# A hybrid decoder step on one core: each delta head as three streams, with a fifth raw projection in the prologue

## The chip, the cores and the metric

The kernel runs on 1 core of a Trainium2 chip. The metric is the device time of one execution in microseconds (us). Five engines work side by side, each with its own in-order queue of instructions: PE (TensorE, matmuls), DVE (VectorE), ACT (ScalarE), POOL (GpSimd) and SP (SyncE, which here only issues DMAs).

## What is computed

One decoder layer on a prompt of 1024 tokens and 8 single-token samples, which the kernel treats as 1032 columns side by side. All is float32. The part that the change touches is branch A, a gated delta rule in 4 heads of 128 by 128, in chunks:

```python
h = rmsnorm(x, norm_g)
aq, ak, av, abeta, aalpha, agate, bu, bv, bgate, cq, cgate, mg = split(h @ w_in)
q, k, v = silu(causal_conv(aq, ak, av))          # 4 taps; q and k are then L2-normed per head
# per head, per chunk (gc = cumulative log decay):
L    = strictly_lower((k * beta) @ k.T * decay)
Tinv = inverse(I + L)                            # unit lower triangular
u, w = Tinv @ (v * beta), Tinv @ (k * beta * exp(gc))
attn = lower(q @ k.T * decay)
def step(S, c):                                  # over the chunks, one after another
    v_new = u[c] - w[c] @ S
    o     = q_dec[c] @ S + attn[c] @ v_new
    return S * g_last[c] + k_dec[c].T @ v_new, o
ya = rmsnorm(o) * silu(agate)
# branches B (spatial MLP on bu, bv, bgate) and C (attention into a memory), then
y = x + (g0 * (ya @ w_a) + g1 * (yb @ w_b) + g2 * (yc @ w_c)) @ w_out   # g = sigmoid(mg + b)
```

Here the chunks have 128 tokens, 8 to a head. The samples' tokens update eight separate states per head (`state_delta`).

## The kernel before

**Projections.** Each column tile of `w_in` (1024 x 128) is a job of PE: `project` runs three float32r products (`whi` x `hTh`, `whi` x `hTl`, `wlo` x `hTh`, which together replace one float32 product) over 8 blocks of depth and 3 column groups of 344, 72 matmuls in all (line L302). ACT and DVE split each weight tile into hi and lo (L277, L280) one job ahead. `plan_a` lists the jobs by name: k, v, q and ag (gate) of the four delta heads, bu, bv, bg of branch B, and gate tiles of the final merge. `plan_c` and `plan_m` follow in later stages.

**What sets the order.** The program is written out by one thread of Python. After every 6 matmuls of a projection `tick()` lets each running generator (`run.add`) go one step, up to its next `yield`; `yield n` skips n ticks. So the instructions of a generator stand in the queues between those of the projections that run at that point, and each engine executes its queue in that order. `run.until` runs generators on until a condition holds.

**Prologue.** Tiles k0, v0, bv0 and q0 are projected from x times g that isn't yet scaled by the root mean square (`raw_group`, four column groups of 256 or 264); DVE multiplies each result by `rbc`, the reciprocal root, on the way out. Then `n_again` splits the scaled h into hi and lo, and the small product for beta and alpha (L652, L653) is the first to use it.

**Delta heads.** `delta_all` runs `gates_gen`, then `delta_gen(h)` for the heads one after another. A head waits for its k, v and q (projection and convolution; the convolution of q runs on POOL, L485 and L487). Then, in this order: transposes of k (L225), E (decay), `LA` (L872: K·K and K·Q of a chunk in one matmul of 256 columns; L873 scales); the four diagonal 32x32 blocks of L go through DRAM (`ld` L883, `Lt` L887) into a layout in which POOL inverts them all at once, in 31 steps of two operations each (L926, L932); `sample_gen(h)` starts before that loop, so its load of `st` (L733) does as well; r (scaled v), the transposes of q and their squares follow. The inverse goes back through DRAM (`ud` L938, `U` L940); after `yield 14`, DVE transposes its blocks (`TA` L943) and small matmuls (from L951) build the full inverse U. Then come the recurrence over 8 chunks (L990 to L1006), the norm, and the turning back (transposes of `r`, DVE L1019 ahead of them). The kernel goes on to branches B and C when head 3 is done.

**Samples.** `sample_gen(h)` norms the samples' q and k, loads `st` (the eight states), multiplies them by q and k on PE, and sends d through DRAM (`ddr` L794, `dbc` L796) to update the states.

Of the kernel before, what the change touches and what calls it, by code (L numbers as in the profile page):

```python
# [151 lines left out]
def tile_mixer_step(ctx: ExitStack, tc: tile.TileContext, a):  # L152
# [576 lines left out]
    def sample_gen(h):  # L729
        kq, vs = kq_s[h]  # L730
# [90 lines left out]
    def delta_gen(h):  # L821
        while not {("k", h), ("v", h), ("q", h), "gates"} <= done:
            yield
        yield 1
        kq, vt = kq_t[h], v_t[h]
        kqs = sm.tile([P, 2, NB], F32, tag="kqs", name="kqs")
        G.tensor_copy(out=kqs, in_=kq[:, :, T:NT])
        vss = sm.tile([P, NB], F32, tag="vss", name="vss")
        G.tensor_copy(out=vss, in_=vt[:, T:NT])
        kq_s[h] = (kqs, vss)  # L830
        gcb = dp.tile([P, CC, P], F32, tag="gcb", name="gcb")
        SP.dma_start(out=gcb, in_=gcd[h * CC:(h + 1) * CC].rearrange("c i -> (c i)").partition_broadcast(P))
        E = dp.tile([P, CC, P], F32, tag="E", name="E")
        ss = sm.tile([P, 2, CC], F32, tag="ss", name="ss")
        Kg = dp.tile([P, CC, P], F32, tag="Kg", name="Kg")
        kd = dp.tile([P, CC, P], F32, tag="kd", name="kd")
        r = dp.tile([P, CC, P], F32, tag="r", name="r")
# [3 lines left out]
        nk = sm.tile([P, CC], F32, tag="nk", name="nk")  # L841
        halves = [slice(0, 4), slice(4, 8)]
        kt = []
        for cs in halves:
            t = dl().rearrange("p (c n) -> p c n", c=4)
            kt.append(t)
            for c in range(4):
                cc = cs.start + c
# [4 lines left out]
            V.tensor_tensor(out=Kg[:, cs], in0=t, in1=bc4(eg[:, h, cs]), op=ALU.mult)
            yield 1
        for c in range(CC):
            V.scalar_tensor_tensor(
                out=E[:, c], in0=gcb[:, c], scalar=gc[:, h, c:c + 1], in1=mask, op0=ALU.subtract, op1=ALU.add
            )
# [8 lines left out]
        yield
        LA = dp.tile([P, 2, CC, P], F32, tag="LA", name="LA")
        for c in range(CC):
            t = dl()[:, :256].rearrange("p (t i) -> p t i", t=2)  # L870
# [1 line left out]
            PE.matmul(t, lhsT=kq[:, 0, sl], rhs=kq[:, :, sl], start=True, stop=True)  # L872
            V.scalar_tensor_tensor(  # L873
                out=LA[:, :, c], in0=t, scalar=cj[:, c:c + 1],
                in1=E[:, c].unsqueeze(1).to_broadcast([P, 2, P]), op0=ALU.mult, op1=ALU.mult,
            )
# [4 lines left out]
        ld = dr.tile([CC, 4, 32, 32], F32, tag="ld", name="ld", bufs=2)
        for b in range(4):
            SP.dma_start(out=ld[:, b].rearrange("c j i -> j c i"), in_=LA[bsl[b], 0, :, bsl[b]])  # L883
# [8 lines left out]
        for cs, t in zip(halves, kt):  # L892
            V.tensor_tensor(out=kd[:, cs], in0=t, in1=bc4(ck[:, cs]), op=ALU.mult)
            yield
        yield from rsqrt_slow(nk, ssk, "nk")
        V.tensor_tensor(out=nk, in0=nk, in1=ssk, op=ALU.mult)
        run.add(sample_gen(h))
        for cs in halves:
            t = dl().rearrange("p (c n) -> p c n", c=4)
            for c in range(4):  # L900
                cc = cs.start + c
                transpose(t[:, c], vt[:, cc * P:(cc + 1) * P])
            V.tensor_tensor(out=r[:, cs], in0=t, in1=bc4(nk[:, cs]), op=ALU.mult)
            yield
        qg = kq[:, 1, :T].rearrange("p (c i) -> p c i", c=CC)
        for cs in halves:
            t = dl().rearrange("p (c n) -> p c n", c=4)
            for c in range(4):
                cc = cs.start + c
                transpose(t[:, c], qg[:, cc])  # L910
            for c in range(4):
                cc = cs.start + c
                S.activation(out=junk(), in_=t[:, c], func=AF.Square, accum_out=ss[:, 1, cc:cc + 1])
            yield 1
        V.tensor_tensor(out=gcb, in0=qg, in1=gcb, op=ALU.mult)
        yield
        ssq = sm.tile([P, CC], F32, tag="ssq", name="ssq")
        V.tensor_scalar(out=ssq, in0=ss[:, 1], scalar1=EPS, scalar2=None, op0=ALU.add)
        rq = sm.tile([P, CC], F32, tag="rq", name="rq")
        yield from rsqrt_slow(rq, ssq, "rq")  # L920
        V.tensor_scalar(out=rq, in0=rq, scalar1=DKS, scalar2=None, op0=ALU.mult)
        yield 2
# [14 lines left out]
        for q in range(4):
            SP.dma_start(out=udv[:, q], in_=X[bsl[q]])  # L938
        for b in range(4):
            SP.dma_start(out=U[bsl[b], :, bsl[b]], in_=ud[:, b].rearrange("c m q i -> (m q) c i"))  # L940
# [9 lines left out]
        for c in range(CC):  # L950
            PE.matmul(t1[b1, c], lhsT=LA[b0, 0, c, b1], rhs=TA[b0, c, b0], start=True, stop=True)  # L951
# [36 lines left out]
        for c in range(CC):  # L988
# [613 lines left out]
```

## Time and profile before

| | us |
|---|---|
| median of 3 runs (lowest to highest) | 1160.41 (1159.37 to 1164.16) |
| profiled execution, its own time | 1163.22 |
| its span | 1161.5 |
| PE busy in the span | 1119.0 (96%) |
| DVE busy | 637.7 (55%) |
| ACT busy | 412.2 (35%) |
| POOL busy | 230.8 (20%) |

The span runs from the first instruction to the last; the execution's own time is 1.7 us longer. PE's busy share says how much of the span no change of the other engines can take away. A row of the timeline gives the start, the duration, the engine (SPq is SP's queue of DMA issues), the line, the operation with output and input, and, in brackets, the idle time before it and what ended it. A row with xN stands for N instructions in succession; since matmuls are pipelined, the price of one is the distance from the start of its row to the start of the next, divided by N.

### The profile page before, as it was taken

The page shows a single profiled execution, that of the slowest core. Times are in us where ns is not written, and L with a number is a line of the kernel's source. Part 1 is how long each engine was busy: PE and PEld are TensorE (multiplying, and loading weights), DVE is VectorE, ACT ScalarE, POOL GpSimd, SP SyncE. Part 2 cuts the span into 40 slices and gives each one's busy share as a digit, 9 for nine tenths or more (in the row PEclk, how much of TensorE's full clock was granted, in tenths as well). Part 3 has the DMA queues.
Part 4 walks back from the last instruction along what each step waited for, and adds up shares of the span by engine and source line. Part 5 has one row for each costly group of instructions (what it writes and reads, how often), then busy time and mean ns, then how long its engine had stood idle before and what let it go on. Part 6 is the DMA issues. An engine that isn't in the chain of part 4 may idle for free.

```text
span 1161.5 us, 19130 instructions
## 1 busy us (share of the span) xinstructions
PE 1119.0 (96%) x7530; PEld 1070.1 (92%) x7530; DVE 637.7 (55%) x1585; ACT 412.2 (35%) x879; POOL 230.8 (20%) x392
## 2 busy tenths in 40 slices
PE   8959999999999999999899999999999999999997
PEld 8948999999999999999799999989999999998884
DVE  5993763477357635722386522645645256786554
ACT  6334332333332233333344323545445321232232
POOL 0043285036504540420034100101101000000000
PEclk8979999999999999999999999899999999999999
DMA  9103321233023302431644455344343365662221
GB/s 366 48 19 75 114 82 39 93 115 93 28 94 114 83 20 93 133 119 55 216 135 140 151 164 193 112 132 127 110 128 92 123 195 178 218 216 92 90 92 56
DMA packets 83033, 137.75 MB, mean 119 GB/s; under 512 B 21744, under 2 KB 51664, under 8 KB 82296
## 3 DMA queue, kind: packets, MB, share of 16 engines
q1 hardware_dynamic: 69392, 95.62, 25.3%
q10 hardware_dynamic: 13552, 40.92, 11.8%
q8 instruction: 59, 0.97, 0.4%
q14 instruction: 30, 0.25, 0.1%
HBM read 104.97 MB, written 31.64 MB: 118 GB/s over the span
## 4 chain that ended last, share of the span: by engine, by line
PE 84%; DVE 8%; DMA 4%; ACT 2%; issue 1%; SPq 0%; ACTq 0%; POOL 0%; DVEq 0%
PE pj L302 49%; PE dl L302 21%; PE tp L225 1%; PE dl L225 1%; PE dl L872 1%; DVE xT L330 1%; PE dl L1220 1%; DMA x<-mem_prompt 1%; PE dl L1006 1%; PE tp L1172 1%; PE dl L982 1%; PE dl L990 1%; PE dl L997 1%; DMA sbg<-g 1%; PE dl L1005 1%
## 5 line engine op out<-in xcount | busy, mean ns | idle before, releaser
L302 PE MATMUL pj<-hTh,whi 128*128 128x344 f32 (+1 forms) x1392 | 273.8, 331 | 9.6 <-DVE ql L188 3.4
L302 PE MATMUL pj<-hTh,wlo 128*128 128x344 f32 (+1 forms) x1392 | 267.1, 326 | 0.0
L302 PE MATMUL pj<-hTl,whi 128*128 128x344 f32 (+1 forms) x1392 | 260.1, 325 | 0.0
L302 PEld LDWEIGHTS pj<-hTh,whi 128*128 128x128 f32 x1392 | 225.3, 191 | 13.9 <-DVE ql L188 3.6
L302 PEld LDWEIGHTS pj<-hTh,wlo 128*128 128x128 f32 x1392 | 225.7, 190 | 1.9 <-issue 1.2
L302 PEld LDWEIGHTS pj<-hTl,whi 128*128 128x128 f32 x1392 | 226.7, 191 | 0.8 <-issue 0.2
L280 DVE TENSOR_TENSOR wlo<-raw,whi 128x1024 fp32r<-128x1024 f32 (+1 forms) x92 | 100.5, 1094 | 44.4 <-ACT whi L277 44.2
L277 ACT CAST whi<-raw 128x1024 fp32r<-128x1024 f32 (+1 forms) x92 | 86.1, 936 | 75.4 <-PE dl L302 64.9
L926 POOL TENSOR_TENSOR itmp<-X,Lt 128x60 f32<-128x60 f32 (+24 forms) x124 | 48.7, 393 | 174.0 <-DMA Lt<-ld 164.7
L1045 ACT COPY stg<-pj 128x344 f32<-128x344 f32 x72 | 32.1, 446 | 121.4 <-PE pj L302 121.3
L1277 POOL TENSOR_TENSOR kvt<-kvt,qb 128x1024 f32<-128x1024 f32 x8 | 19.2, 2418 | 214.6 <-DMA kvt<-cache_mem_v 214.6
L302 PE MATMUL dl<-yl,whi 128*128 128x344 f32 x288 | 57.2, 320 | 0.0
L302 PE MATMUL dl<-yh,wlo 128*128 128x344 f32 x288 | 57.1, 320 | 0.0
L302 PE MATMUL dl<-yh,whi 128*128 128x344 f32 x288 | 56.9, 319 | 0.0
L932 POOL TENSOR_TENSOR X<-X,itmp 128x60 f32<-128x60 f32 (+24 forms) x124 | 54.3, 438 | 9.7
L302 PEld LDWEIGHTS dl<-yl,whi 128*128 128x128 f32 x288 | 47.6, 188 | 0.0
L302 PEld LDWEIGHTS dl<-yh,whi 128*128 128x128 f32 x288 | 47.5, 188 | 0.0
L302 PEld LDWEIGHTS dl<-yh,wlo 128*128 128x128 f32 x288 | 47.4, 188 | 0.0
L994 DVE COPY y<-dl 128x128 f32<-128x128 f32 x32 | 9.3, 291 | 61.3 <-PE dl L992 40.1
L1460 DVE TENSOR_TENSOR stg<-dl,stg 128x344 f32<-128x344 f32 x48 | 24.7, 514 | 17.7 <-PE dl L302 17.7
L487 POOL TENSOR_TENSOR kq<-kq,cvt 128x512 f32<-128x512 f32 x24 | 33.4, 1392 | 1.9
L516 ACT COPY xraw<-pj 128x344 f32<-128x344 f32 x27 | 12.0, 444 | 59.9 <-PE pj L302 59.9
(389 smaller groups left out, 1669.6 us busy)
## 6 DMA issues: line engine op xcount, KB each, us to landing
raw<-w_tiles ACTq DMA_DIRECT2D x62, 512.0 KB
gate<-stg SPq DMA_DIRECT2D x23, 516.0 KB
stg<-gate SPq DMA_DIRECT2D x23, 516.0 KB
raw<-w_br ACTq DMA_DIRECT2D x24, 256.0 KB
x<-x_prompt SPq DMA_DIRECT2D x8, 512.0 KB
kvt<-cache_mem_k SPq DMA_DIRECT2D x16, 256.0 KB
kvt<-cache_mem_v SPq DMA_DIRECT2D x16, 256.0 KB
wor<-w_out SPq DMA_DIRECT2D x8, 512.0 KB
```

The lines of the kernel that those rows point to most:

```text
L225: PE.transpose(out, in_, ident[:p, :p])
L277: S.copy(out=hi, in_=raws[i])
L280: eng.tensor_tensor(out=lo, in0=raws[i], in1=f32(hi), op=ALU.subtract)
L302: PE.matmul(out, lhsT=w, rhs=r, start=(i == 0), stop=(i == len(ops) - 1))
L330: V.scalar_tensor_tensor(out=x[:, k], in0=x[:, k], scalar=colv[:, col + k:col + k + 1], in1=r, op0=ALU.mult, op1=ALU.mult)
L487: G.tensor_tensor(out=d[:, cs], in0=d[:, cs], in1=o, op=ALU.add)
L516: S.copy(out=raw[:, 3 + sl.start:3 + sl.stop], in_=o)
L926: G.tensor_tensor(out=tm, in0=X[:, 0:m, j:j + 1].to_broadcast([P, m, n]), in1=Lt[:, j:j + 1, j + 1:32].to_broadcast([P, m, n]), op=ALU.mult,)
L932: G.tensor_tensor(out=X[:, 0:m, j + 1:32], in0=X[:, 0:m, j + 1:32], in1=tm, op=ALU.subtract)
L1045: project("gate", i, lambda n, sl, o: S.copy(out=t[:, sl], in_=o))
L1277: G.tensor_tensor(out=kts[hb], in0=kts[hb], in1=qb[:, hb * 4:hb * 4 + 4].unsqueeze(2).to_broadcast([P, 4, 2, P]), op=ALU.mult,)
L1460: V.tensor_tensor(out=sg[:, sl], in0=o, in1=sg[:, sl], op=ALU.mult)
```

## The change

`delta_gen` is cut in three generators. `inverse_gen(h)` waits for k alone. It computes K·K (L860, two-pass float32 of 128 columns) into `L`; the squares of k, which ACT summed from the transposed k, are now the diagonal of K·K (DVE multiplies by the identity and reduces). Then come E, L, `ld`, `Lt`, POOL's loop (L901, L907), `ud`, `U` and the small matmuls (from L929). `chunks_gen(h)`, started ahead of the loop, does the transposes of k, K·Q (L998) into `A`, the transposes of q and v. `chain_gen(h)` does the recurrence and the turning; when it starts, `inverse_gen(h + 1)` starts as well. Flags ("dbc", "rec", "turned", "chunks") keep the buffers of two heads apart: `Lt` takes the buffer of the samples' `dbc`, the diagonals that of `p2`. `sample_gen(h)` is added after POOL's loop instead of before it. k, v and q of a head are projected only when the chunks of the head before are done.

`plan_a` is put in another order, with 8 gates at the end instead of 1 + 7. In the prologue a fifth tile, bv1, is projected from x g in the four column groups of the others, and `n_again` moves behind q0 into bv1's loop.

```diff
@@ plan_a
-        [("k", 0), ("v", 0), ("bv", 0), ("q", 0), ("ag", 0), ("bv", 1), ("bv", 2)],
-        [("k", 1), ("v", 1), ("q", 1), ("ag", 1), ("bv", 3), ("bg", 0), ("bu", 0)] + gates(1),
-        [("k", 2), ("v", 2), ("q", 2), ("ag", 2), ("bg", 1), ("bu", 1), ("bg", 2), ("bu", 2)],
-        [("k", 3), ("v", 3), ("q", 3), ("ag", 3), ("bg", 3), ("bu", 3)] + gates(7),
+        [("k", 0), ("v", 0), ("bv", 0), ("q", 0), ("bv", 1), ("ag", 0), ("bv", 2), ("bv", 3), ("bg", 0)],
+        [("k", 1), ("v", 1), ("q", 1), ("bu", 0), ("ag", 1), ("bg", 1), ("bu", 1)],
+        [("k", 2), ("v", 2), ("q", 2), ("bg", 2), ("ag", 2), ("bu", 2), ("bg", 3)],
+        [("k", 3), ("bu", 3), ("v", 3), ("q", 3), ("ag", 3)] + gates(8),
@@ prologue
         e_q(NS - 1 if n == 3 else 0, part[n], held.pop((n, 0)), False)
-        n_again(n)
...
+    w = splits.pop(4)
+    bv1 = stage()
+    for n in range(4):
+        raw_group(n, 0, w)
+        V.tensor_tensor(out=bv1[:, part[n]], in0=held.pop((n, 0)), in1=rbc[:, part[n]], op=ALU.mult)
+        n_again(n)
+        if n == 2:
+            for _ in w_split(5, slow=False):
+                pass
             split(wab2[:, :, 0:8], wab2[:, :, 8:16], wab)
+    SP.dma_start(out=bv_d[1], in_=bv1)
@@ inverse_gen(h)
+        while ("k", h) not in done:
             yield
...
+            t = bank()
             for c in range(4):
+                k = kq[:, 0, (cs.start + c) * P:(cs.start + c + 1) * P]
+                PE.matmul(t[:, c], lhsT=k, rhs=k, start=True, stop=True)
+            S.copy(out=L[:, cs], in_=t)
...
+            d = dp.tile([P, 4, P], F32, tag="p2", name="diag")
+            V.tensor_tensor(out=d, in0=L[:, cs], in1=ident.unsqueeze(1).to_broadcast([P, 4, P]), op=ALU.mult)
+            V.tensor_reduce(out=ssk[:, cs], in_=d, axis=AX.X, op=ALU.add)
...
+            SP.dma_start(out=ld[:, b].rearrange("c j i -> j c i"), in_=L[bsl[b], :, bsl[b]])
+        while h and ("dbc", h - 1) not in done:
+            yield
+        Lt = dp.tile([P, 32, 32], F32, tag="dbc", name="Lt")
...
-        run.add(sample_gen(h))
...
+        run.add(chunks_gen(h))
+        yield 8
         for j in range(31):
...
+        run.add(sample_gen(h))
         ud = dr.tile([CC, 4, 8, 4, 32], F32, tag="ud", name="ud", bufs=2)
...
             SP.dma_start(out=udv[:, q], in_=X[bsl[q]])
+        while h and ("rec", h - 1) not in done:
+            yield
         for b in range(4):
             SP.dma_start(out=U[bsl[b], :, bsl[b]], in_=ud[:, b].rearrange("c m q i -> (m q) c i"))
         yield 14
...
+        while ("chunks", h) not in done:
+            yield
         yield 1
+        if h + 1 < H:
+            run.add(inverse_gen(h + 1))
+        run.add(chain_gen(h))
+
+    def chunks_gen(h):
+        while h and ("rec", h - 1) not in done:
+            yield
...
+                PE.matmul(t[:, c], lhsT=kq[:, 0, sl], rhs=kq[:, 1, sl], start=True, stop=True)
...
+        while h and ("turned", h - 1) not in done:
+            yield
+        r = dp.tile([P, CC, P], F32, tag="r", name="r")
...
@@ job(kind, i)
         if kind in ("k", "v", "q"):
+            run.until(lambda: i == 0 or ("chunks", i - 1) in done)
             project(kind, i, qkv_tile(kind, i))
```

SP's queue in head 0 before, from the way of L to POOL (`ld`, `Lt`) to the way of the inverse back (`ud`, `U`); `st` are the samples' states, `ddr` and `dbc` their d, `bv` a projected tile:

```order
L883 DMA ld<-LA 32x8x32 x4
L887 DMA Lt<-ld 32x1024 x4
L733 DMA st<-state_delta 128x8x128
L1067 DMA bv_144<-stg 128x1032
L794 DMA ddr<-drow 8x128
L796 DMA dbc<-ddr 128x1024
L473 DMA conv_new<-xraw 128x11
L810 DMA sd_sample<-st 128x8x128
L938 DMA ud<-X 256x1x32 x4
L940 DMA U<-ud 32x8x32 x4
```

The same in the changed kernel:

```order
L885 DMA ld<-L 32x8x32 x4
L891 DMA Lt<-ld 32x1024 x4
L1129 DMA bv_144<-stg 128x1032
L969 DMA gcb<-gcd 128x1024
L1129 DMA bv_145<-stg 128x1032
L914 DMA ud<-X 256x1x32 x4
L918 DMA U<-ud 32x8x32 x4
L745 DMA st<-state_delta 128x8x128
L806 DMA ddr<-drow 8x128
L808 DMA dbc<-ddr 128x1024
```

The load of `st` and the samples' two transfers have moved from ahead of `ud` and `U` to behind them.

PE in the changed kernel, head 2, between the transposes of q (`kq`) and the first matmul of the inverse's blocks (L929); L771 multiplies the samples' states `st` by their k and q (`kqp`):

```order
L225 MATMUL dl<-ident,kq 128x128 x4
L302 MATMUL pj<-hTh,whi 128x344 x6
L771 MATMUL tp<-st,kqp 32x128 x8
L302 MATMUL pj<-hTh,whi 128x344 x2
L302 MATMUL pj<-hTl,whi 128x344 x4
L225 MATMUL tp<-ident,rr 128x128 x2
...
L302 MATMUL pj<-hTl,whi 128x344 x4
L302 MATMUL pj<-hTh,wlo 128x344 x8
L929 MATMUL dl<-TA,L 32x32
```

L771 comes ahead of L929 there, with 42 projection matmuls and some transposes between them. In heads 0 and 1 it does too, in head 3 it comes after. Before, the samples' matmul stood ahead of the first one of the blocks (L951) in every head as well, but its load did not stand behind the inverse on SP.

POOL before, head 3: the end of q's convolution (L485, L487) and the start of the loop of the inverse (L926, L932):

```order
L485 TENSOR_TENSOR cvt<-xraw,colv 128x512
L487 TENSOR_TENSOR kq<-kq,cvt 128x512
L827 COPY kqs<-kq 128x16
L829 COPY vss<-vt 128x8
L889 MEMSET X 128x256
L891 MEMSET X 32x8 x4
L926 TENSOR_TENSOR itmp<-X,Lt 128x31
L932 TENSOR_TENSOR X<-X,itmp 128x31
```

In the changed kernel, head 3, the 41st operation of the loop:

```order
L901 TENSOR_TENSOR itmp<-X,Lt 128x60
L907 TENSOR_TENSOR X<-X,itmp 128x5x12
L485 TENSOR_TENSOR kq<-xraw,colv 128x512 x2
L485 TENSOR_TENSOR cvt<-xraw,colv 128x512
L487 TENSOR_TENSOR kq<-kq,cvt 128x512
```

The convolution of q3 has moved from ahead of the loop into it, behind 40 of its 62 operations. In heads 1 and 2 the convolution of q still stands ahead of the loop, in head 0 it is over long before.

More of the change, by code (lines that the diff above doesn't have):

```diff
@@ L729, in sample_gen @@
     def sample_gen(h):
+        while h not in kq_s:
+            yield
         kq, vs = kq_s[h]
@@ L810, in sample_gen @@
         SP.dma_start(out=a["sd_sample"][:, h].rearrange("b k v -> k b v"), in_=st)
+        done.add(("dbc", h))
         while ("ag", h) not in done:
@@ L819, in junk, with bank, inverse_gen @@
         return dp.tile([P, P], F32, tag="junk", name="junk", bufs=2)
-    def delta_gen(h):
-        while not {("k", h), ("v", h), ("q", h), "gates"} <= done:
+    halves = [slice(0, 4), slice(4, 8)]
+    bsl = [slice(32 * b, 32 * b + 32) for b in range(4)]
+    b0, b1, b2, b3 = bsl
+    hd = {}
+    def bank():
+        return dl().rearrange("p (c n) -> p c n", c=4)
+    def inverse_gen(h):
+        hd[h] = {}
+        E = dp.tile([P, CC, P], F32, tag="E", name="E")
+        SP.dma_start(out=E, in_=gcd[h * CC:(h + 1) * CC].rearrange("c i -> (c i)").partition_broadcast(P))
+        while ("k", h) not in done:
             yield
         yield 1
[L825 to L837, printed above, removed]
+        kq = kq_t[h]
+        L = dp.tile([P, CC, P], F32, tag="L", name="L")
         ssk = sm.tile([P, CC], F32, tag="ssk", name="ssk")
@@ L891, in delta_gen @@
             G.memset(X[bsl[q]].rearrange("p m i -> p (m i)")[:, q:256:36], 1.0)
[L892 to L896, printed above, removed]
-        run.add(sample_gen(h))
[L898 to L922, printed above, removed]
+        run.add(chunks_gen(h))
+        yield 8
         for j in range(31):
@@ L969, in delta_gen @@
         for c in range(CC):
-            PE.matmul(t1[hi_, c], lhsT=LA[lo_, 0, c, hi_], rhs=TA[:, c], start=True, stop=True)
+            PE.matmul(t1[hi_, c], lhsT=L[lo_, c, hi_], rhs=TA[:, c], start=True, stop=True)
         S.mul(out=p2[hi_], in_=t1[hi_], mul=-1.0)
@@ L976, in delta_gen @@
         V.tensor_copy(out=U[lo_, :, hi_], in_=t1[lo_])
+        while ("chunks", h) not in done:
+            yield
         yield 1
+        if h + 1 < H:
[3 more added lines that the diff above has]
+        while h and ("rec", h - 1) not in done:
+            yield
+        kq, vt = kq_t[h], v_t[h]
+        E, ssk, cj, ck = (hd[h][n] for n in ("E", "ssk", "cj", "ck"))
+        gcb = dp.tile([P, CC, P], F32, tag="gcb", name="gcb")
+        SP.dma_start(out=gcb, in_=gcd[h * CC:(h + 1) * CC].rearrange("c i -> (c i)").partition_broadcast(P))
+        Kg = dp.tile([P, CC, P], F32, tag="Kg", name="Kg")
+        kd = dp.tile([P, CC, P], F32, tag="kd", name="kd")
+        A = dp.tile([P, CC, P], F32, tag="A", name="A")
+        hd[h].update(gcb=gcb, Kg=Kg, kd=kd, A=A)
+        for cs in halves:
+            t = bank()
+            for c in range(4):
+                cc = cs.start + c
+                transpose(t[:, c], kq[:, 0, cc * P:(cc + 1) * P])
+            V.tensor_tensor(out=Kg[:, cs], in0=t, in1=bc4(eg[:, h, cs]), op=ALU.mult)
+            V.tensor_tensor(out=kd[:, cs], in0=t, in1=bc4(ck[:, cs]), op=ALU.mult)
+            yield 1
+        S.activation(out=gcb, in_=gcb, func=AF.Exp)
+        nk = sm.tile([P, CC], F32, tag="nk", name="nk")
+        yield from rsqrt_slow(nk, ssk, "nk")
+        V.tensor_tensor(out=nk, in0=nk, in1=ssk, op=ALU.mult)
+        while not {("q", h), ("v", h)} <= done:
+            yield
+        yield 1
+        kqs = sm.tile([P, 2, NB], F32, tag="kqs", name="kqs")
+        G.tensor_copy(out=kqs, in_=kq[:, :, T:NT])
+        vss = sm.tile([P, NB], F32, tag="vss", name="vss")
+        G.tensor_copy(out=vss, in_=vt[:, T:NT])
+        kq_s[h] = (kqs, vss)
+        for cs in halves:
+            t = bank()
+            for c in range(4):
+                sl = slice((cs.start + c) * P, (cs.start + c + 1) * P)
+                PE.matmul(t[:, c], lhsT=kq[:, 0, sl], rhs=kq[:, 1, sl], start=True, stop=True)
+            for c in range(4):
+                cc = cs.start + c
+                V.scalar_tensor_tensor(
+                    out=A[:, cc], in0=t[:, c], scalar=cj[:, cc:cc + 1], in1=E[:, cc], op0=ALU.mult, op1=ALU.mult
+                )
+            yield 1
+        qg = kq[:, 1, :T].rearrange("p (c i) -> p c i", c=CC)
+        ssq = sm.tile([P, CC], F32, tag="ssq", name="ssq")
+        for cs in halves:
+            t = bank()
+            for c in range(4):
+                transpose(t[:, c], qg[:, cs.start + c])
+            for c in range(4):
+                cc = cs.start + c
+                S.activation(out=junk(), in_=t[:, c], func=AF.Square, accum_out=ssq[:, cc:cc + 1])
+            yield 1
+        V.tensor_tensor(out=gcb, in0=qg, in1=gcb, op=ALU.mult)
+        yield
+        V.tensor_scalar(out=ssq, in0=ssq, scalar1=EPS, scalar2=None, op0=ALU.add)
+        rq = sm.tile([P, CC], F32, tag="rq", name="rq")
+        yield from rsqrt_slow(rq, ssq, "rq")
+        V.tensor_scalar(out=rq, in0=rq, scalar1=DKS, scalar2=None, op0=ALU.mult)
+        while h and ("turned", h - 1) not in done:
+            yield
+        r = dp.tile([P, CC, P], F32, tag="r", name="r")
+        hd[h].update(r=r, rq=rq)
+        for cs in halves:
+            t = bank()
+            for c in range(4):
+                cc = cs.start + c
+                transpose(t[:, c], vt[:, cc * P:(cc + 1) * P])
+            V.tensor_tensor(out=r[:, cs], in0=t, in1=bc4(nk[:, cs]), op=ALU.mult)
+            yield
+        done.add(("chunks", h))
@@ L978, in delta_gen, with chain_gen @@
+    def chain_gen(h):
+        gcb, Kg, kd, A, r = (hd[h][n] for n in ("gcb", "Kg", "kd", "A", "r"))
         wT = Kg
         for cs in halves:
-            t = dl().rearrange("p (c n) -> p c n", c=4)
+            t = bank()
             for c in range(4):
@@ L1005, in delta_gen @@
                 PE.matmul(t, lhsT=gcb[:, c], rhs=Sc, start=True, stop=False)
-            PE.matmul(t, lhsT=LA[:, 1, c], rhs=y, start=(c == 0), stop=True)
+            PE.matmul(t, lhsT=A[:, c], rhs=y, start=(c == 0), stop=True)
             S.copy(out=o_t[:, c], in_=t)
@@ L1038, in delta_all @@
         yield from gates_gen()
-        for h in range(H):
-            yield from delta_gen(h)
+        run.add(inverse_gen(0))
     def gate_tile(i, t):
@@ L1079, in tile_mixer_step @@
     run.add(delta_all())
-    for kind, i in sum(plan_a, [])[4:]:
+    for kind, i in sum(plan_a, [])[5:]:
         job(kind, i)
```

67 lines of the change are left out of this document (24 added, 43 removed).

## The prediction

> **What bounds the kernel now.** I read the shares of busy time first, then the chain that ended last, then TensorE's waits, then the timeline around each wait.
>
> ```profile
> PE 1119.0 (96%) x7530; PEld 1070.1 (92%) x7530; DVE 637.7 (55%) x1585; ACT 412.2 (35%) x879; POOL 230.8 (20%) x392
> PE 84%; DVE 8%; DMA 4%; ACT 2%; issue 1%; SPq 0%; ACTq 0%; POOL 0%; DVEq 0%
> PE pj L652 <- DVE wab L188: 12.1, 1, 12.1
> PE dl L225 <- DVE r L1019: 4.6, 1, 4.6
> PE pj L302 <- ACT stg L1066: 2.1, 1, 2.1
> PE dl L872 <- DVE LA L873: 0.6, 1, 0.6
> PE dl L951 <- DVE TA L943: 0.5, 1, 0.5
> ```
>
> TensorE (PE) is busy 96% of the span and 84% of the chain. So the time is PE's work plus its waits, and the change can win only the few waits listed (line, what it waited for, us in total, times, longest). The largest two:
>
> ```profile
> 77.57 0.21 DVE L188 TENSOR_TENSOR wab<-wab,wab 128x64 fp32r<-128x64 f32 x1
> 77.83 0.47 PE L652 MATMUL pj<-hTh,wab 128*16 128x344 f32 x1 [12.13 <-DVE wab L188]
> 559.41 1.94 PE L225 MATMUL dl<-ident,r 128*128 128x128 f32 x8 [4.58 <-DVE r L1019]
> 561.00 2.24 PE L302 MATMUL pj<-hTh,whi 128*128 128x344 f32 x8
> 563.08 1.43 PE L302 MATMUL pj<-hTl,whi 128*128 128x344 f32 x8
> 564.35 1.44 PE L302 MATMUL pj<-hTh,wlo 128*128 128x344 f32 x8
> ```
>
> The first is in the prologue: PE waits until DVE has split wab. The second is the drain after head 3: plan_a has run out of projections. The last four rows also give PE's prices. From start to start, eight 344-column matmuls take 1.27 us (563.08 to 564.35), 0.158 each. The eight right after the wait take 2.08, and the eight transposes 1.59. Prices for the others:
>
> ```profile
> 552.60 0.38 PE L990 MATMUL dl<-r,U 128*128 128x128 f32 x2
> 552.82 0.39 PE L992 MATMUL dl<-S,Kg 128*128 128x128 f32 x2
> 121.09 1.02 PE L872 MATMUL dl<-kq 128*128 128x256 f32 x4
> 121.76 0.67 PE L302 MATMUL pj<-hTh,whi 128*128 128x344 f32 x2
> 109.63 0.60 PE L225 MATMUL dl<-ident,kq 128*128 128x128 f32 x4
> 109.99 0.40 PE L302 MATMUL pj<-hTl,whi 128*128 128x344 f32 x1
> ```
>
> A row of two L990 is one fp32 matmul in two passes: 0.22. With 256 columns (L872) it is 0.67/2 = 0.335, a transpose 0.36/4 = 0.09. Eight transposes at 0.09 are 0.72, so the wait at 559 cost 4.6, and 0.87 + 0.81 = 1.7 more of slow matmuls behind it. I charge 1.7 behind every new wait of several us.
>
> The inverse chain decides the rest. Head 0 on DVE, SP, POOL:
>
> ```profile
> 117.37 2.18 DVE L856 SCALAR_TENSOR_TENSOR E<-gcb,gc,mask 128x128 f32<-128x128 f32 x8
> 127.31 0.87 DVE L873 SCALAR_TENSOR_TENSOR LA<-dl,cj,E 128x256 f32<-128x256 f32 x2
> 128.20 1.80 SPq L883 DMA_DIRECT2D ld<-LA  x4
> 131.36 2.09 SPq L887 DMA_DIRECT2D Lt<-ld  x4
> 133.50 0.43 SPq L733 DMA_DIRECT2D st<-state_delta  x1
> 135.77 0.24 POOL L926 TENSOR_TENSOR itmp<-X,Lt 128x31 f32<-128x31 f32 x1 [27.66 <-DMA Lt<-ld]
> 169.19 0.21 POOL L932 TENSOR_TENSOR X<-X,itmp 128x8 f32<-128x8 f32 x1
> 169.43 2.64 SPq L938 DMA_DIRECT2D ud<-X  x4
> ```
>
> From the end of LA (128.2) to POOL's start 7.6 us pass, then the 62 operations take 33.6, and ud is issued when the last of them has ended. In head 3 and after head 1 the same steps:
>
> ```profile
> 466.40 0.92 DVE L873 SCALAR_TENSOR_TENSOR LA<-dl,cj,E 128x256 f32<-128x256 f32 x2 [0.89 <-PE dl L872]
> 477.04 0.24 POOL L926 TENSOR_TENSOR itmp<-X,Lt 128x31 f32<-128x31 f32 x1 [44.97 <-DMA Lt<-ld]
> 478.02 1.10 POOL L932 TENSOR_TENSOR X<-X,itmp 128x30 f32<-128x30 f32 x1
> 502.81 0.21 POOL L932 TENSOR_TENSOR X<-X,itmp 128x8 f32<-128x8 f32 x1
> 280.01 1.21 POOL L932 TENSOR_TENSOR X<-X,itmp 128x8 f32<-128x8 f32 x1
> 281.25 2.54 SPq L938 DMA_DIRECT2D ud<-X  x4
> 285.23 1.82 SPq L940 DMA_DIRECT2D U<-ud  x4
> 286.94 0.43 DVE L943 STREAM_TRANSPOSE TA<-U 32x256 f32<-32x256 f32 x1 [3.12 <-DMA U<-ud]
> ```
>
> Head 3: 9.7 to POOL's start, 26.0 on POOL. From POOL's end to the transposes of U: 5.7 (281.2 to 286.94). The convolution of q runs on POOL too:
>
> ```profile
> 173.15 1.04 POOL L485 TENSOR_TENSOR kq<-xraw,colv 128x512 f32<-128x512 f32 x1 [2.59 <-ACT xraw L516]
> 188.08 1.27 POOL L487 TENSOR_TENSOR kq<-kq,cvt 128x512 f32<-128x512 f32 x1
> ```
>
> That is 16.2 us. Before, no PE instruction depends on a recent POOL end: all of this is covered, since L951 waited only 0.5 us.
>
> **The change, part by part.** Counts of instructions are from the order of the changed program.
>
> *SP's queue.* sample_gen is now added after the POOL loop, so the load of st (L745) stands on SP behind ud (L914) and U (L918), which wait for X. What is queued behind them is st, ddr and dbc. PE needs st at L771, which in heads 0, 1 and 2 stands ahead of L929, the first user of the finished inverse. So in these heads PE waits at L771, in head 3 at L929. From POOL's end to st: the issues of ud and U with the landing between them, 0.1 + 2.5 + 1.5 + 1.8 = 5.8 (281.2 to 287.05), st's issue 0.4, and its landing; the nearest row is Lt, issued until 133.45 and used at 135.77, 2.3 to 2.5. Together 8.7.
>
> *Head 0.* The start is the last K·K (L860). L must then be copied by ACT, its two half diagonals multiplied and reduced, and L scaled: four 128x512 operations at 0.87 (the rate of 127.31), 8 scalings of 128x128 at 2.18/8, some 1.5 for the copy and the exponential, and a split or two of DVE's other work between them: 8 us, between 5.5 without any other work and 10. The POOL loop has two ends, 26.0 and 33.6. I take 28, nearer the faster: once PE waits, DVE gets no new work and POOL has the rate of head 3. Need: 8 + 7.6 + 28 + 8.7 = 52.3. Cover on PE up to L771: 216 projections x 0.158, 24 transposes x 0.09, 8 K·Q x 0.22 and a little: 38.3. Wait 14 (8 to 22).
>
> *Heads 1 and 2.* The convolution of q stands ahead of the inverse on POOL, so the clock starts at the end of q's projection: 0.5 + 16.2 + 28 + 8.7 = 53.4. Cover in head 1: 186 projections, 25 two-pass and 8 K·Q matmuls at 0.22, 24 transposes: 39.1, wait 14.3 (12 to 20). In head 2: 174 projections, 8 transposes, 8 K·Q: 30.2, wait 23.2 (21 to 29).
>
> *Head 3.* The convolution of q stands in the middle of the 62 operations. Need from the last L860 to L929: 7 + 7.6 + 28 + 16.2 + 5.7 + 0.5 = 65; cover 270 projections, 16 transposes, 4 K·Q: 45. Wait 20 (11 to 28). L771 comes later there and waits for nothing.
>
> *The sum of waits* is 71.5, and 4 x 1.7 = 6.8 of slow matmuls behind them.
>
> *K·K and K·Q apart*: 64 matmuls at 0.22 for 32 at 0.335: +3.4. The wait at L872 (0.6) goes.
>
> *The recurrence* now runs beside the next head's inverse; its y copies on DVE queue behind that head's E and L work. No row shows it. Bounds: 0 (the copies were never waited for) and 8 (32 steps, each behind one 0.27 operation); I take 3, nearer the end of the rows without a wait.
>
> *The drain* (4.6 + 1.7 = 6.3) goes: after head 3's recurrence more than eight gate projections are left. *Small waits* (0.6 + 0.5): -1.1.
>
> *The prologue.* bv1 costs the same matmul columns there as in plan_a: nothing. It stands ahead of L652, but DVE gets its evacuations and another split ahead of wab's, and the convolution of q0 on POOL, now behind no other work, doesn't come sooner; the wait is mostly moved, gain 2 (0 to 6: half of 12.1). ACT's wait at 112.6 (stg L1066, 2.1) lies behind the same loads: gain 2 (0 to 3.8).
>
> Sum: 71.5 + 6.8 + 3.4 + 3 - 6.3 - 1.1 - 2 - 2 = +73.3. The profiled execution took 1163.2 (span 1161.5 and 1.7 around it), 2.8 above the median of 1160.4. So 1236.5 profiled, 1234 as a median.
>
> **A rule against a row.**
>
> ```profile
> L280 DVE TENSOR_TENSOR wlo<-raw,whi 128x1024 fp32r<-128x1024 f32 (+1 forms) x92 | 100.5, 1094 | 44.4 <-ACT whi L277 44.2
> ```
>
> The row at 478.02 takes 1.10 where its neighbours take 0.24, and loops of the same 62 operations took 26.0 and 33.6: POOL slows while DVE works. The Trainium skill, "SBUF — State Buffer", section "Who interferes with whom", says why: a DVE instruction with two SBUF inputs contends with a GpSimd instruction that reads SBUF, and the one that comes second is blocked for the whole of the first. Here DVE's splits (two SBUF inputs) are such instructions, and the trace agrees: 1.10 is the length of one split (92 of them, mean 1094 ns). By that rule the change, which puts scalings of L, diagonals and recurrence beside the loop, would slow it further; the sum by the rule would be the third rival's.
>
> **Rivals.** *1. Everything is hidden (the other side):* the order leaves PE more cover than I count, or st lands early; then only K·K, the recurrence and the gains remain: 73.3 - 78.3 = -5, 1155 (1146 with all of the gains, 1163 without). For it: L951 waited only 0.5 before. Against: in head 2 the cover must be 53 us instead of 30, and POOL's loop itself would have to end in 5. It decides if PE's distance from q's projection to L771 exceeds 53 us in all heads.
>
> *2. st doesn't bind, only U does:* if st's buffer were loaded in time, PE would wait at L929: st's issue and landing and the order ahead of it fall out of the sum, and by the cover up to L929 (47.5, 47.3, 38.4 and 45 us) the waits are 1.8, 3.6, 12.5 and 20, sum 37.9, two slow stretches 3.4; 1163.2 + 37.9 + 3.4 + 6.4 - 11.4 - 2.8 = 1197. Against: SP issues in order (133.50 follows Lt's issues at once).
>
> *3. POOL at its slow rate in every head:* +5.6 x 4, and Lt at 9.7 instead of 7.6 in heads 0 and 3: +26.6, 1260. For it: 33.6 in head 0. Against: 26.0 in head 3.
>
> **How the numbers follow.** Chances: main case 0.76 (1205 to 1258: the loop at its fast end in every head takes 8 off, at 32 adds 16, and the recurrence and the prologue move it by some 8 more), rival 1 0.09, rival 2 0.08, rival 3 0.07. The range 1194 to 1264 holds the main case, half of rival 2 and most of rival 3. Faster by over 0.5% (below 1154.6; less than that a measurement here can't tell from no change) is about half of rival 1: 0.05; within 0.5%: 0.04; slower: 0.91.
>
> **What would show it.** In the changed profile: PE waits at L771 for st of some 14, 14 and 23 us in heads 0 to 2 and at L929 of some 20 in head 3, SP waiting for POOL's X ahead of L914, no drain before the branch stage, and slow matmuls after each wait. Wrong if the waits at L771 are short, if PE waits in the recurrence by more than 8 us, or if the prologue's wait vanishes altogether.

## The result, and the profile after

The changed kernel took 1252.24 us (median of 4 runs, 1251.64 to 1252.42) against 1160.37: a ratio of 1.0784, interval 1.076 to 1.0809. The forecast was 1234 in a range of 1194 to 1264. The profiled execution took 1252.3, its span is 1250.6 us, 89.1 longer than before. First the page's busy shares, the granted clock in 40 slices, and the chain that ended last:

```profile
PE 1141.1 (91%) x7618; PEld 1091.1 (87%) x7618; DVE 644.5 (52%) x1637; ACT 411.8 (33%) x824; POOL 209.9 (17%) x392
PEclk8979988888988899879999999999999999999999
PE 69%; POOL 10%; DVE 9%; DMA 6%; issue 3%; SPq 2%; ACT 2%; POOLq 0%; DVEq 0%; ACTq 0%
```

PE is 22.1 us busier than before, and 67.0 us more of the span are idle on PE. The clock row (tenths of full speed) has eights and a seven between slices 6 and 18, the delta heads, where it was nine throughout; from slice 19 on it is nine again. Between 156 and 563 us the granted clock was 0.90, against 1.00 before. In the chain PE fell from 84% to 69%, and POOL, which had 0%, has 10%.

PE's waits, the rows that this text uses (line, what it waited for, us in total, times, longest):

```profile
PE tp L752 <- DVE pr L749: 23.5, 2, 17.0
PE pj L302 <- ACT xraw L516: 15.1, 2, 9.4
PE tp L771 <- DMA st<-state_delta: 14.7, 3, 8.6
PE pj L662 <- DVE wab L188: 8.3, 1, 8.3
PE dl L929 <- DVE TA L921: 7.9, 1, 7.9
PE pj L302 <- ACT stg L1128: 4.1, 2, 3.2
PE dl L998 <- ACT kq L499: 3.9, 1, 3.9
PE dl L1056 <- DVE y L1053: 3.7, 2, 3.5
PE dl L938 <- DVE pn L932: 2.2, 1, 2.2
```

The drain of 4.6 is gone, and the wait for wab is 8.3 instead of 12.1, with a new one of 3.2 for wlo ahead of it. Nearly all of the rest is new. Head 2 shows the largest, in rows of the timeline of POOL, DVE, PE and SP:

```profile
386.41 1.28 POOL L487 TENSOR_TENSOR kq<-kq,cvt 128x512 f32<-128x512 f32 x1
409.55 0.21 POOL L907 TENSOR_TENSOR X<-X,itmp 128x8 f32<-128x8 f32 x1
409.70 0.20 POOL L990 COPY kqs<-kq 128x16 f32<-128x16 f32 x1
409.93 0.17 DVE L747 TENSOR_TENSOR pr<-kqs 128x8 f32<-128x8 f32 x1 [18.24 <-POOL kqs L990]
410.30 0.62 PE L752 MATMUL tp<-pr,ones 128*128 128x24 f32 x2 [17.00 <-DVE pr L749]
416.14 0.46 SPq L745 DMA_DIRECT2D st<-state_delta  x1
420.31 0.64 PE L771 MATMUL tp<-st,kqp 128*32 128x128 f32 x16 [1.58 <-DMA st<-state_delta]
```

The convolution of q ends on POOL at 387.7 and the loop at 409.8. Right behind it stands kqs, the copy of the samples' q and k: 0.20 us of work that L752 waited 17.0 for. Then st lands 10 us after the loop's end and costs 1.6 more. Ahead of this, in the same head, on SP, ACT and PE:

```profile
358.42 1.80 SPq L885 DMA_DIRECT2D ld<-L  x4
361.60 1.71 SPq L891 DMA_DIRECT2D Lt<-ld  x4
363.82 0.43 SPq L969 DMA_DIRECT2D gcb<-gcd  x1
369.06 1.06 ACT L982 ACTIVATE gcb<-gcb 128x1024 f32<-128x1024 f32 x1 [6.32 <-DMA gcb<-gcd]
370.02 0.43 ACT L516 COPY xraw<-pj 128x344 f32<-128x344 f32 x1
370.50 1.80 PE L302 MATMUL pj<-hTh,whi 128*128 128x344 f32 x5 [9.36 <-ACT xraw L516]
```

The second broadcast gcb is issued behind ld and Lt, which wait for L. ACT stands at the exponential of gcb until it lands, xraw's copy stands behind it, and PE has no free bank: 9.4 us. The same happens in head 0 (3.2, under stg L1128) and in head 3 (5.7).

### The profile page after: what moved, and what is told of

Read it like the earlier page. It is cut to its first block, busy times and chain, and to the rows that moved or that the text cites. A ratio compares the mean times of both kernels' runs of the same rounds, so it can differ in the third digit from the quotient of the medians.

```text
span 1250.6 us, 19297 instructions
## 1 busy us (share of the span) xinstructions
PE 1141.1 (91%) x7618; PEld 1091.1 (87%) x7618; DVE 644.5 (52%) x1637; ACT 411.8 (33%) x824; POOL 209.9 (17%) x392
## 3 DMA queue, kind: packets, MB, share of 16 engines
q1 hardware_dynamic: 70112, 98.24, 24.3%
## 4 chain that ended last, share of the span: by engine, by line
PE 69%; POOL 10%; DVE 9%; DMA 6%; issue 3%; SPq 2%; ACT 2%; POOLq 0%; DVEq 0%; ACTq 0%
PE pj L302 38%; PE dl L302 20%; POOL itmp L901 3%; POOL X L907 3%; POOL kq L487 2%; POOL cvt L485 2%; PE tp L225 1%; DVE xT L330 1%; DMA st<-state_delta 1%; DVE hTl L188 1%; PE dl L1282 1%; DMA ud<-X 1%; DVE vt L494 1%; DVE wlo L280 1%; SPq L918 1%
## 5 line engine op out<-in xcount | busy, mean ns | idle before, releaser
L302 PE MATMUL pj<-hTh,whi 128*128 128x344 f32 (+1 forms) x1384 | 275.8, 336 | 25.6 <-ACT xraw L516 15.1
L302 PE MATMUL pj<-hTl,whi 128*128 128x344 f32 (+1 forms) x1384 | 263.7, 328 | 0.0
L302 PEld LDWEIGHTS pj<-hTh,whi 128*128 128x128 f32 x1384 | 229.3, 197 | 30.0 <-ACT xraw L516 15.6
L1106 ACT COPY stg<-pj 128x344 f32<-128x344 f32 x72 | 32.1, 446 | 125.2 <-PE pj L302 125.2
L901 POOL TENSOR_TENSOR itmp<-X,Lt 128x60 f32<-128x60 f32 (+24 forms) x124 | 39.4, 318 | 81.5 <-DMA Lt<-ld 72.3
L907 POOL TENSOR_TENSOR X<-X,itmp 128x60 f32<-128x60 f32 (+24 forms) x124 | 38.9, 314 | 9.7
L487 POOL TENSOR_TENSOR kq<-kq,cvt 128x512 f32<-128x512 f32 x24 | 35.9, 1498 | 1.9
L1066 ACT COPY r<-dl 128x128 f32<-128x128 f32 x32 | 8.5, 266 | 83.4 <-PE dl L1065 80.8
```

What stands on the lines that cost most here:

```text
L302: PE.matmul(out, lhsT=w, rhs=r, start=(i == 0), stop=(i == len(ops) - 1))
L487: G.tensor_tensor(out=d[:, cs], in0=d[:, cs], in1=o, op=ALU.add)
L901: G.tensor_tensor(out=tm, in0=X[:, 0:m, j:j + 1].to_broadcast([P, m, n]), in1=Lt[:, j:j + 1, j + 1:32].to_broadcast([P, m, n]), op=ALU.mult,)
L907: G.tensor_tensor(out=X[:, 0:m, j + 1:32], in0=X[:, 0:m, j + 1:32], in1=tm, op=ALU.subtract)
L1106: project("gate", i, lambda n, sl, o: S.copy(out=t[:, sl], in_=o))
```

## Experiments

Ratios are to the kernel before, timed beside each set on the same chip. The table gives the median, the ratio with its interval, and PE's idle time, worked out for all from one rule (distance between an end and the next start; 32.3 before, 99.1 after); it is that of the profiled execution, not of the median. The kernel before had medians of 1160.4 to 1163.0 us in these sets, so 3 us between rows of different sets say little. E12 was run last.

| | median, us | ratio (95%) | PE idle, us |
|---|---|---|---|
| changed kernel | 1252.2 | 1.0784 (1.0760 to 1.0809) | 99.1 |
| E1 gcb late | 1247.1 | 1.0725 (1.0696 to 1.0754) | 95.4 |
| E2 no loop | 1191.5 | 1.0239 (1.0205 to 1.0272) | 50.4 |
| E3 st and kqs | 1235.6 | 1.0618 (1.0585 to 1.0651) | 84.7 |
| E12 st alone | 1240.0 | 1.0677 (1.0656 to 1.0699) | 93.5 |
| E4 convolution on DVE | 1203.3 | 1.0343 (1.0313 to 1.0373) | 60.3 |
| E5 = E1 + E3 + E4 | 1181.4 | 1.0153 (1.0117 to 1.0188) | 41.1 |
| E6 wab early | 1248.9 | 1.0743 (1.0699 to 1.0787) | 97.1 |
| E7 old prologue | 1250.7 | 1.0746 (1.0706 to 1.0787) | 103.5 |
| E8 = E5 + E6 | 1177.3 | 1.0116 (1.0074 to 1.0157) | 38.3 |
| E9 = E8, longer pauses | 1162.7 | 1.0005 (0.9987 to 1.0022) | 32.0 |
| E10 before + wab early | 1159.3 | 0.9979 (0.9958 to 0.9999) | 31.8 |
| E11 = E10 + a gate | 1160.7 | 0.9983 (0.9964 to 1.0001) | 28.2 |

**E2: is it POOL's chain?**

```diff
         for j in range(31):
+            if j:
+                if j % 2 == 1:
+                    yield
+                continue
```

> Leaves out 60 of the 62 operations of POOL's loop in each head (the inverse of the diagonal blocks is not computed); the order of everything else stays. Theory (the chain from POOL's loop through kqs, ud, U and st ends PE's waits): the loop ends some 24 us earlier in each head, PE's waits at L771 (8.6 in head 0), at L752 and L771 (10.9 in head 1, 18.6 in head 2) and at L998, L929, L930 (12.6 in head 3) go, 50.7 in all, with some 10 us of slow matmuls behind them: 1191 (1183 to 1200). Rival (the DMAs in a row on SP and ACT's queue end them, not POOL): 1235 to 1252.

It took 1191.5, the theory's number. Two of the waits that are left, the longest one and what remains for st:

```profile
PE pj L302 <- ACT xraw L516: 15.0, 2, 9.2
PE tp L771 <- DMA st<-state_delta: 0.3, 1, 0.3
```

L752, L929 and L998 have no row any more, and L771 has 0.3. The wait for xraw stays at 15.0: it does not depend on POOL. So POOL's loop carries 50 us of waits and with what follows them 61 of the 92.

**E4: the loop, or what stands ahead of it?**

```diff
-        if key[0] == "q":          # ... four taps on POOL (L485, L487)
+        if True:                   # q as k and v: on DVE
```

> The convolution of q runs on DVE, in the form of k's and v's, instead of POOL. Theory (in heads 1 to 3 POOL's chain is late since the convolution of 17 us and the loop of 24 to 27 stand one after the other on POOL): the waits of heads 1 and 2 at L752 and L771 (29.5) go, head 3's 12.6 falls to 2 or less, head 0 keeps 8.6; 40 us of waits and 9 of slow matmuls less: 1203 (1195 to 1215). Rival (DVE, with 5 us more in each head, gets late with the splits of weights and the y of the recurrence): waits of PE for wlo and y appear, 1225 to 1250.

1203.3, again the theory's number. The loop is still there, with the same 62 operations a head, and yet 49 us are gone. DVE was not late: PE's wait for wlo is 2.5 (3.2 in the changed kernel), for y 3.7 as there. In heads 1 to 3 the loss is therefore mainly the row of convolution and loop on POOL: without the loop (E2) the convolution hides, and without the convolution the loop does in heads 1 and 3. Left of the chain are head 0's wait for st (8.3) and, in head 2, 0.9 at L742 and 4.2 for st:

```profile
PE tp L761 <- DMA st<-state_delta: 12.5, 2, 8.3
PE tp L742 <- DVE pr L739: 0.9, 1, 0.9
380.54 1.08 PE L761 MATMUL tp<-st,kqp 128*32 128x128 f32 x16 [4.22 <-DMA st<-state_delta]
```

**E3 and E12: st, or kqs?**

```diff
+        st = dp.tile([P, NB, P], F32, tag="st", name="st")      # behind Lt's load, ahead of the loop
+        SP.dma_start(out=st, in_=a["state_delta"][:, h].rearrange("b k v -> k b v"))
...
-        G.tensor_copy(out=kqs, in_=kq[:, :, T:NT])              # E3 only, and the same for vss
+        V.tensor_copy(out=kqs, in_=kq[:, :, T:NT])
```

> st is loaded right behind Lt, ahead of the loop, and the two small copies kqs and vss run on DVE instead of POOL, so that of the samples nothing waits for POOL's loop. Theory (in heads 0 to 2 the samples' path binds, and the inverse alone would bind later): waits at L752 and L771 go, L929 waits some 0, 1 and 9 us in heads 0 to 2, head 3 keeps its 12.6: 28 us of waits and 6 of slow matmuls less, 1218 (1210 to 1228). Rival (U ends the wait as late as st did): 1243 to 1253.

> The changed kernel with st loaded right behind Lt, ahead of the loop, alone: kqs and vss stay on POOL. The prediction had put all of the waits in heads 0 to 2 on st. Theory (st binds in head 0 alone; in heads 1 and 2 kqs, behind the loop on POOL, would hold PE at L752 without st as well): the waits at L771 (8.6, 4.5, 1.6) go, those at L752 (6.5 and 17.0) stay, and gcb, now behind st on SP, lands some 2 us later in heads 0, 2 and 3: 1242 (1238 to 1248), 6 or more above the run that moved st and kqs together (1235.6). Rival (st ends the waits, L752 only shows them first): 1233 to 1237, and the waits at L752 shrink.

With st alone (E12):

```profile
PE tp L751 <- DVE pr L748: 23.6, 2, 17.1
PE pj L302 <- ACT xraw L516: 18.5, 2, 10.7
```

The waits for kqs are what they were (23.5, longest 17.0), L771's wait for st has gone, and the time is 12 less, although the waits at ACT's queue (xraw and stg) have grown by 6.5. kqs binds in heads 1 and 2 on its own. With both (E3) U is what is late:

```profile
PE pj L302 <- ACT xraw L516: 19.1, 2, 11.4
PE dl L931 <- DVE TA L923: 18.4, 2, 9.4
PE tp L770 <- DVE kqp L761: 8.9, 2, 7.0
```

9 us in head 2, as expected, and 9.4 in head 3. But E3 missed its range by 8: 7.0 us of wait in head 1 for the samples' own norm, and 7 more at ACT's queue, because st, now ahead of gcb on SP, delays it. A load moved out of one wait lengthened another.

**E1: ACT behind gcb.** The exponential moves from behind the transposes of k to just before its first use.

> Theory A (a cost of its own that the prediction had not seen: ACT stands at the exponential of gcb until its load lands, SP issues that load behind ld and Lt, and PE runs out of free PSUM banks): with the exponential moved to just before its first use, PE's waits at L302 for ACT's copy of xraw (9.4 us in head 2, 5.7 in head 3) go. Head 2's comes off the time with some 4 us of slow matmuls behind it, since q's convolution there starts earlier too; head 3's is taken up again by its later wait at L929. Time 1238 (1234 to 1244). Rival (POOL's chain ends all the waits, whatever stands before): the waits at L752 and L929 grow by what is saved, 1249 to 1254.

1247.1: between the two. The waits for xraw fall from 15.1 to 0.7, but of the 18.3 us (with head 0's 3.2) only 5 reach the end:

```profile
PE tp L752 <- DVE pr L749: 23.8, 2, 17.4
PE tp L771 <- DMA st<-state_delta: 20.6, 3, 14.1
PE dl L997 <- ACT kq L499: 9.1, 1, 9.1
```

Head 0's 3.2 and head 3's 5.7 went into later waits (L771 from 8.6 to 14.1; L997 from 3.9 to 9.1), since POOL ends these. Only head 2's came through, where q's convolution starts earlier too: from head 1 to head 2 E1 gains 8.3 us on the changed kernel (by the starts of L771). It had lost 1.4 by head 1, and loses 1.9 again at the samples' norm of head 3 (L800).

**E5 and E8: all of it.** E5 joins E1, E3 and E4; E8 adds E6's edit.

> The three edits together: the exponential of gcb just before its use, st loaded ahead of the loop with kqs and vss copied on DVE, the convolution of q on DVE. Theory (the three causes, POOL's row of convolution and loop, SP's order, ACT behind gcb's load, make up the loss): no wait of PE over 2 us between the first K·K and the end of head 3 but the y of the recurrence (3.5) and pn (2.2); of the loss of 90 us what stays is K·K and K·Q apart (3.4), these two and some slow matmuls: 1168 (1160 to 1178). Rival (the waits move on to DVE, which now has the convolutions of q, the copies and the recurrence): 1185 to 1205.

> The three edits of the first run of this set and the early split of wab. Theory: some 8 below the first of this set, 1160 (1152 to 1170), about the time of the kernel before or a little under it. Rival (the prologue's gain is lost again in the first head): the same time as the first, within 2.

E5 missed its range by 3, E8 by 7, and between them lie 4 us of the 8 expected, with intervals that overlap. PE's idle time is down to 41.1 and 38.3, but not to before's 32.3; in E8:

```profile
PE dl L922 <- DVE TA L914: 9.4, 3, 6.0
PE tp L790 <- DVE rs_t L197: 4.7, 3, 1.9
PE dl L1049 <- DVE y L1046: 3.6, 2, 3.5
```

Before, only U's had rows, of 0.5 and 0.2. The reading of them is distance: with three streams in turn, fewer projections stand between a result and its use. E9 tests it.

**E9: more distance.** E8 with `yield 20` for 14 ahead of U's transposes, 2 for 1 behind pn, 3 for 1 ahead of the samples' last product.

> The three edits and the early split of wab, and three pauses lengthened: 20 ticks instead of 14 between U and its transposes, 2 instead of 1 behind pn, 3 instead of 1 ahead of the samples' last product. Theory (what is left of PE's waits at U 11.3, at the samples' norm 4.7, at pn 2.2 is distance on PE alone, and head 3 has gates enough behind it): 16 less, 1160 (1154 to 1168) beside 1163 of before. Rival (head 3 gets late and the drain comes back, or the waits move to the recurrence): 1172 to 1182.

1162.7 beside 1162.3: the time of the kernel before, within 0.2%. The waits at U are down to 1.5, part of them returned as others (y 6.9, r 4.8):

```profile
PE dl L1049 <- DVE y L1046: 6.9, 3, 2.9
PE dl L225 <- DVE r L1073: 4.8, 2, 2.5
```

So with its own losses taken away the changed kernel is level with the one before. E9 has the early split of wab, though, and the kernel before gets it too in E10, timed in the same set: 1159.3, 3.5 us below E9, with intervals that overlap. No run shows the three streams winning anything.

**E6 and E7: the prologue.** E6 splits wab ahead of the first `n_again`; E7 has the prologue of before (four raw tiles).

> The changed kernel with one edit: DVE splits wab ahead of the first n_again instead of behind the split of the next weights. Theory (PE's wait at L662 is DVE's order: wab comes last of five things): the wait of 8.3 falls to 2 or less, the slow stretch behind it shortens: 1244 (1241 to 1249). Rival (the hTl products end as late as wab does, or the time saved is taken up by head 0's wait at L771): 1250 to 1254.

> The changed kernel with the prologue of before (four raw tiles, bv1 projected as the job behind q0). The prediction took 2 us for the gain of the fifth tile. Theory (the wait is only moved): 1250 to 1256. Rival (the fifth tile fills a wait of 12): 1258 to 1266.

E7's ratio, 1.0746 (1.0706 to 1.0787), is not above the changed kernel's: the fifth tile gained nothing at the end. Its wait for wab is 12.3, longer by 4 (3.2 of them the changed kernel spends ahead of it, at wlo), its wait for st in head 0 is 14.5 instead of 8.6, and in head 1 it has waits of 4.8 (for stg) and 3.7 (for r), where the changed kernel has none and 0.6. Yet by head 2 the two stand level: the matmul behind pr starts at 409.7 in E7 and at 410.3 in the changed kernel. E6 brought the wait at L662 from 8.3 to pieces of 0.6 to 2.8 at hTl (L664, 5.6 in all), and 3 us of time by the medians, with intervals that overlap: inconclusive on the time, clear on the wait.

**E10 and E11: the same gains in the kernel before.** E10 is the kernel before with the early split of wab; E11 moves one gate tile from the end of plan_c to the end of plan_a as well.

> The kernel before with one edit: DVE splits wab ahead of the first n_again instead of behind the last but one and a split of weights. Theory (the wait of 12.1 at L652 is DVE's order, and nothing behind it has time to give back): 3 to 5 of the wait stay for hTl, 8 go with about 2 of slow matmuls: 1153 (1150 to 1157). Rival (gates and decay come earlier, but K K waits for the convolution of q0 anyway): 1160 to 1164.

> The kernel before with the early split of wab and one gate tile more at the end of plan_a, taken from the end of plan_c. Theory (the drain of 4.6 with 1.7 of slow matmuls is a lack of one job of 11.4): 6 below the run before it in this set, 1147 (1143 to 1153). Rival (the gate tile covered a wait at the end of plan_c as long as the drain): the same time as that run, within 2, or more.

Both miss: 3 and 2 us less than before, where 9 and 15 were expected. E10's interval ends at 0.9999 and E11's holds 1; that E11 takes no less than E10 is what its rival said. In E10 the 12.1 became mainly these:

```profile
68.62 0.47 PE L654 MATMUL pj<-hTl,wab 128*16 128x344 f32 x1 [4.36 <-DVE hTl L188]
74.20 0.32 PE L653 MATMUL pj<-hTh,wab 128*16 128x344 f32 x1 [1.73 <-DVE xraw L518]
```

4.4 and 1.7 of it for DVE's other work, and among the waits, for the decay's chain on DVE, where before 0.6 were left:

```profile
PE tp L702 <- DVE gp L698: 4.7, 1, 4.7
```

In E11 the drain is gone, and where the gate tile was taken away a wait opens:

```profile
895.00 0.44 PE L225 MATMUL tp<-ident,p 128*128 128x128 f32 x2 [2.60 <-ACT pb L1242]
896.16 0.44 PE L225 MATMUL tp<-ident,p 128*128 128x128 f32 x2 [0.73 <-DVE sum L1246]
```

E10 has the lowest median of the case, 0.2% below the kernel before, which is about what these runs can tell apart.

## Why the prediction was right, point by point

Direction and size of the loss were right, and so was its main cause, POOL's chain; the place was right in head 0 and, but for 3.9 us at L998, in head 3. The closeness of the sum is in part luck: POOL's waits were put 20.8 us too high, and 18.3 us of waits for ACT and 13 us of slow matmuls were missing from it. By the prediction's own sign (wrong if the waits at L771 are short) it failed in heads 1 and 2: they are 4.5 and 1.6 us.

| term | predicted | measured |
|---|---|---|
| POOL's chain, heads 0 to 3 | 14, 14.3, 23.2, 20: 71.5 | 8.6, 10.9, 18.6, 12.6: 50.7 |
| ACT behind gcb, heads 0, 2, 3 | not seen | 3.2, 9.4, 5.7: 18.3 |
| slow matmuls behind waits | 6.8 | 20 |
| K·K and K·Q apart | 3.4 | 2 |
| recurrence | 3 | 3.7 (y) |
| the inverse's pn, head 0 | not seen | 2.2 |
| drain | -6.3 | -4.6 of wait; its 1.7 are in the 20 |
| prologue | -2 | 0 (E7) |
| ACT's wait for stg behind the prologue | -2 | -1.2 (0.9 left) |

*POOL's chain.* The lengths were good: in head 0, from the last K·K (125.2) to L771 (177.4) 52.2 us passed, where 52.3 was the sum. Here too errors cancel: up to the loop 17.4 us passed instead of 15.6, the loop took 24.2 instead of 28, and from its end to L771 it was 10.6 instead of 8.7. In heads 1 and 2 it was some 53 and 50 from the end of q's projection, where the sum had 53.4, in head 3 67.3 up to L929 instead of 65. The mis-sized term is the cover, by these lengths less the waits: 43.6, 42.5, 31.7 and 55.5 us, where the count of its matmuls gave 38.3, 39.1, 30.2 and 45. PE had waited for ACT in it in heads 0 and 3 (3.2 and 5.7); that the rest is slow matmuls behind other waits is not shown by a run. In heads 1 and 2 the prediction put the wait on st at L771. That step failed in the main: it read what is queued behind the loop on SP, and not what is queued behind it on POOL. kqs stands there, and L752 needs it. E12 shows it: without st's wait, L752 still waits 6.5 and 17.1.

*ACT.* This was the step left out. Under SP's queue the text named st, ddr and dbc as what stands behind a wait. gcb was in the same excerpt of SP's order (L969, behind ld and Lt), and ACT's exponential waits for it ahead of xraw's copies. E1 and E2 show it as a cost of its own: E2 takes POOL away and it stays (15.0). Beside POOL's chain, only 5 us of the 18.3 reach the end (E1).

*Slow matmuls.* The prediction counted 4 waits. Between the first K·K and the end of head 3 there are 11 of 2 us or more, and several shorter ones; 20 us over these 11 are 1.8 each, near the 1.7. That the 20 are slow matmuls is read from the busy time, which rose by 22.1 with K·K 2 of it, and from the granted clock of 0.90; no run separates them. These rows give four matmuls, eight passes, in 0.81 us, 0.20 each.

```profile
122.36 1.05 PE L860 MATMUL dl<-kq 128*128 128x128 f32 x8
123.17 1.19 PE L302 MATMUL pj<-hTh,wlo 128*128 128x344 f32 x6
```

*Recurrence.* The term was near, and its reason was right: the copy of y stands on DVE behind the next head's work on L, and once PE waits for it by 3.5 us. The wait for pn (2.2) is no part of the recurrence; it stands in the inverse of head 0.

```profile
220.85 1.14 DVE L878 SCALAR_TENSOR_TENSOR L<-L,cj,E 128x128 f32<-128x128 f32 x4
221.90 0.28 DVE L1053 COPY y<-dl 128x128 f32<-128x128 f32 x1
222.33 0.77 PE L1056 MATMUL dl<-y,kd 128*128 128x128 f32 x2 [3.54 <-DVE y L1053]
```

*Prologue.* "Mostly moved" was right, and 2 us too much: E7 shows no gain at the end.

*The rivals.* Rival 2 (only U binds) is what E3 made: 9.1 us in head 2, where it had 12.5, and 9.4 in head 3, where it had 20. Rival 3, POOL at its slow rate, fell. The groups of the loop's operations after (busy, mean ns):

```profile
L901 POOL TENSOR_TENSOR itmp<-X,Lt 128x60 f32<-128x60 f32 (+24 forms) x124 | 39.4, 318 | 81.5 <-DMA Lt<-ld 72.3
L907 POOL TENSOR_TENSOR X<-X,itmp 128x60 f32<-128x60 f32 (+24 forms) x124 | 38.9, 314 | 9.7
```

and the same two before:

```profile
L926 POOL TENSOR_TENSOR itmp<-X,Lt 128x60 f32<-128x60 f32 (+24 forms) x124 | 48.7, 393 | 174.0 <-DMA Lt<-ld 164.7
L932 POOL TENSOR_TENSOR X<-X,itmp 128x60 f32<-128x60 f32 (+24 forms) x124 | 54.3, 438 | 9.7
```

393 and 438 ns became 318 and 314; the loops took 24.2, 24.3 and 22.1 us in heads 0 to 2 and 26.9 in head 3 (without the convolution inside it), not 28. While PE waits, DVE gets no splits: in head 2, the shortest loop, DVE stood idle for 18.2 us up to kqs (the row at 409.93), and no split fell into it. In E9, where PE hardly waits, the means are up again at 331 and 395, though DVE has the convolutions of q as well there. The Trainium skill, "SBUF — State Buffer", section "Who interferes with whom", has DVE instructions with two SBUF inputs contend with GpSimd instructions that read SBUF; the runs agree with it. They also show the other side: where PE waits for the loop on POOL, DVE gets less work that could slow that loop.

## What to carry to other kernels

Before a step is put behind a long one on any queue, list what else stands behind it on that queue, on every engine, down to the 0.2 us copies: here a copy on POOL, a load on SP and an exponential on ACT held PE for up to 17.0, 8.6 and 9.4 us. When PE is busy 96%, cutting a chain in parallel streams has little to win (32.3 us of waits in all, in the profile before), and three streams left less distance between a result and its use (E9). A wait that is removed ahead of a chain on another engine can come back at that chain (E1 in heads 0 and 3, E10 at the decay's chain): sum the gains only along the chain that ends last.

## What the runs showed that was not expected

Many short waits cost almost a third more in slow matmuls: 67 us more of idle time came with about 20 us of them. And POOL's loop, of 62 small operations, took 33.6 us in head 0 before and 24.2 after, with less work of DVE beside it, so that the duration of a stage on POOL is not a property of that stage alone.
